# Input norm folded into the weights, x loaded early, query and key heads transposed in pairs, queries copied across partitions inside SBUF

## The chip, the cores and the metric

One NeuronCore of one Trainium2 chip. The metric is the device time of one launch in microseconds; a median over several runs is given where there are several.

## The reference

One layer of a hybrid decoder. The prompt has 2048 rows of 1024 (16 blocks of 128 rows); the sample batch adds 8 x 8 = 64 rows, treated as one more block (SB). All of it is float32.

```
h = rmsnorm(x, norm_in_g)             # per row, then times a gain per column
z = h @ w_in                          # 1024 x 3656, split into:
q, k, v, qi, ki, wi, ga, u, vm, gm
q, k = rope(rmsnorm(.)) per head      # 8 query heads, 4 key heads, 64 wide
qi, ki = rope(.)                      # indexer: 8 heads x 64, one key of 64
score = sum_h wi[h] * relu(qi[h] . ki)     # per query and key, causal
top 256 keys per query -> attention over them, times silu(ga)
gelu(u) * (spatial mix of layernorm(gelu(vm))) * silu(gm)
r = x + concat(.) @ w_out
y = r + sigmoid(rmsnorm(r) @ w_ple_gate) * (p @ w_ple_proj)
```

Returned are y for prompt and sample, and the new k, v, indexer keys and gated rows.

## The kernel before

Each float32 operand of a large product is split into a high half (float32r, rounded) and a low half (the rest), and a product is the sum of high x high, high x low and low x high.

**Phase A** makes the projections. `ROUNDS` groups the 17 blocks into three rounds of 6, 6 and 5; within a round the loop runs over the 14 column chunks of `CH` (x1, x2, vm0, vm1, k, v, ...), and within a chunk over the blocks. `load_w` (L264) brings a chunk's weights: in round 0 as eight raw pieces, each split into `whi` (GpSimd, for the first chunk every second one on ScalarE, L282 to L284) and `wlo` (L285: VectorE for the first six pieces, GpSimd for the last two), and both halves are then written to DRAM (L287); later rounds read the halves back (L273). `load_x` (L222) brings a block of x into one of two buffers; `norm_h` (L232) makes the sum of squares (ScalarE, L241), the inverse root (GpSimd, L242 and L243) and x times that times the gain (VectorE, L244); `split_h` (L246) transposes the normalised block in eight 128x128 tiles (L254) and splits it into `hhi` and `hlo` (`split`, L121: ScalarE copy, VectorE subtraction). `proj` (L301) runs 24 matmuls per prompt block and chunk, 16 for SB. `post` (L341) evacuates each chunk's result: indexer, query, key, value and gate parts, in part written to DRAM scratch (`s_qi`, `s_q`, `s_ga`). Between the blocks, `pump` (L446) feeds in the indexer: `idx` (L647) for a block of queries, with `load_qi` (L636), which loads each head's 64 columns twice side by side, so that a transpose puts the head on partitions 0 to 63 and again on 64 to 127. The key tile `ki_stack` holds the key's high half on partitions 0 to 63 and its low half on 64 to 127, so one matmul of 128 rows makes two of the three products. The scores are summed into a `big` tile that begins as a ramp made from `iota` (L663), and `topk` (L785) finds the threshold and writes a mask.

The end of phase A multiplies the gMLP part by half of w_out, and `prep_early` (L951) prepares attention beside it: keys are doubled on ScalarE (`twice`, L997), four transposes (L1005) and a split give `Kst`; `load_q` and `prep_q` do the same for queries (L1013), eight transposes (L1020).

**Phase B** is attention, block after block, four steps (pairs of heads) per block: scores (L1087, L1088), mask and minimum (L1089), exponential (L1096), transposes of the probabilities (L1122), their split, and the product with the values (L1139), with the sample block's attention woven in. `prep_q` of the next block follows a block's third step (L1212). **Phase C** is the output projection and the gate.

All loads and stores but the gathers go through one queue, SP's, in order. The order on each engine and queue is fixed before the run by the framework's planner (`schedule_with_timeline_sim=True`): it plays the program with estimated durations, and where an instruction isn't ready there, one that comes later in the program may go first. Each engine then runs its list in order. So the first ramp (`iota`, L491) stands in the trace ahead of the first norm, which the program has first.

## Time and profile before

| | |
|---|---|
| median of 3 runs | 1916.15 us (1910.57 to 1916.78) |
| profiled execution | 1912.54 us, span 1910.8 us |
| mean granted TensorE clock | 0.987 |
| TensorE busy | 1839.7 us, 96% |
| VectorE, ScalarE, GpSimd busy | 1254.9, 990.2, 632.3 us |
| moved by DMA | 262 MB, 137 GB/s in the mean |
| phase A, B, C end | about 1060, 1570, 1911 us |

The granted clock is 1.00 where TensorE has its upper level (2.4 GHz) and falls towards 0.5 (1.2 GHz) where it has the lower one. The busy time of TensorE holds the overlap of pipelined matmuls, so a mean of one matmul is longer than its share of the stream.

### The profile page before, as it was taken

What the parts mean: (1) busy time and instruction counts of PE and PEld (TensorE: products, weight loads), DVE (VectorE), ACT (ScalarE), POOL (GpSimd) and SP (SyncE); (2) the same over time, 40 slices, a digit from 0 to 9 for tenths busy, and PEclk for the clock granted to TensorE, in tenths of its full rate; (3) what the DMA queues carried; (4) which work ended last, traced back from release to release, by engine and by line L of the source; (5) the groups of instructions that cost most, each with busy time, mean ns of one, the idle gap of its engine ahead of it and who ended that gap; (6) DMA issues with size and microseconds to landing.
All of it is one profiled execution on the core that took longest, in us unless ns stands there. A gap on an engine that the chain in (4) does not pass through costs nothing. (4 is left out here: it accounts for less than half of the span.)

```text
span 1910.8 us, 34742 instructions
## 1 busy us (share of the span) xinstructions
PE 1839.7 (96%) x12374; PEld 1623.1 (85%) x12374; DVE 1254.9 (66%) x3612; ACT 990.2 (52%) x1909; POOL 632.3 (33%) x961
## 2 busy tenths in 40 slices
PE   5989998999999999999999899999999989999998
PEld 5989978999999999999998677778777777888887
DVE  5497745558779648788852689879888866233321
ACT  3234334345565625666764788868877653222221
POOL 4483563324003225005403443242222165222211
PEclk8999999999999999999999999999999999999999
DMA  8755666544444655445554433242322074222311
GB/s 256 226 155 179 197 197 219 182 128 144 130 145 157 222 159 163 149 147 163 168 191 150 133 105 89 65 119 65 82 61 65 20 267 133 85 95 94 103 36 45
DMA packets 242769, 262.10 MB, mean 137 GB/s; under 512 B 82136, under 2 KB 208672, under 8 KB 242208
## 3 DMA queue, kind: packets, MB, share of 16 engines
q1 hardware_dynamic: 236704, 240.97, 40.3%
q0 software_dynamic: 5888, 18.88, 3.3%
q8 instruction: 98, 1.61, 0.3%
q14 instruction: 79, 0.65, 0.1%
HBM read 172.42 MB, written 87.37 MB: 136 GB/s over the span
## 5 line engine op out<-in xcount | busy, mean ns | idle before, releaser
L314 PE MATMUL z<-whi,hhi 128*128 128x256 f32 (+1 forms) x1792 | 461.5, 291 | 11.6 <-ACT vt L408 3.6
L315 PE MATMUL z<-wlo,hhi 128*128 128x256 f32 (+1 forms) x1792 | 455.9, 288 | 1.9 <-POOL wlo L285 1.9
L314 PEld LDWEIGHTS z<-whi,hhi 128*128 128x128 f32 x1792 | 343.8, 192 | 19.9 <-issue 7.2
L315 PEld LDWEIGHTS z<-wlo,hhi 128*128 128x128 f32 x1792 | 344.2, 192 | 5.6 <-POOL wlo L285 2.4
L317 PE MATMUL z<-whi,hlo 128*128 128x256 f32 (+1 forms) x1792 | 270.3, 288 | 0.0
L317 PEld LDWEIGHTS z<-whi,hlo 128*128 128x128 f32 x1792 | 241.8, 191 | 4.2
L677 DVE SCALAR_TENSOR_TENSOR big<-dots,sgn,big 128x1024 f32<-128x1024 f32 (+7 forms) x176 | 179.3, 1019 | 58.0 <-ACT dots L675 56.9
L675 ACT ACTIVATE dots<-dots 128x1024 f32<-128x1024 f32 (+7 forms) x176 | 140.6, 802 | 109.1 <-PE dots L673 104.6
L124 DVE TENSOR_TENSOR b_pt<-b_tp,b_pt 128x512 fp32r<-128x512 f32 (+1 forms) x288 | 183.3, 656 | 11.8 <-ACT b_pt L123 10.2
L1139 PE MATMUL b_o<-b_pt,Vst 128*128 128x512 f32 x544 | 184.5, 424 | 0.9 <-DVE b_pt L124 0.7
L123 ACT ACTIVATE b_pt<-b_tp 128x512 fp32r<-128x512 f32 (+1 forms) x288 | 155.5, 579 | 47.6 <-PE b_tp L1122 41.6
L1122 PE MATMUL b_tp<-mats,b_sm 128*128 128x128 f32 x1088 | 170.6, 274 | 4.0 <-ACT b_sm L1096 2.7
L813 ACT ACTIVATE bfw<-big,tk 128x384 bf16<-128x384 f32 (+14 forms) x105 | 136.5, 1300 | 62.0 <-DVE tk L833 35.3
L1096 ACT ACTIVATE b_sm<-b_sm,b_st 128x128 f32<-128x128 f32 (+15 forms) x128 | 154.7, 1210 | 19.2 <-DVE b_st L1089 18.1
L1122 PEld LDWEIGHTS b_tp<-mats,b_sm 128*128 128x128 f32 x1088 | 132.4, 141 | 33.7 <-ACT b_sm L1096 6.9
L1087 PE MATMUL b_s<-Kst,b_qh 128*128 128x512 f32 (+3 forms) x320 | 140.2, 440 | 8.4 <-DVE b_st L1089 5.3
L1089 DVE CUSTOM_DVE_ANT_0 b_sm<-b_s,b_mask,b_st 128x512 f32<-128x512 f32 (+3 forms) x192 | 124.0, 646 | 25.9 <-PE b_s L1088 19.0
L1088 PE MATMUL b_s<-Kst,b_ql 128*128 128x512 f32 (+3 forms) x320 | 117.1, 369 | 0.0
L672 PE MATMUL dots<-ki_stack,qih 128*128 128x512 f32 (+3 forms) x304 | 111.6, 370 | 1.8 <-DVE big L677 1.8
L1139 PEld LDWEIGHTS b_o<-b_pt,Vst 128*128 128x128 f32 x544 | 90.1, 190 | 23.6 <-DVE b_pt L124 6.9
L673 PE MATMUL dots<-ki_stack,qil 128*128 128x512 f32 (+3 forms) x304 | 109.7, 371 | 0.0
L1449 PE MATMUL c_mm<-c_h_w_ple_gate,c_mh 128*128 128x512 f32 x272 | 109.0, 401 | 0.0
(347 smaller groups left out, 3847.1 us busy)
## 6 DMA issues: line engine op xcount, KB each, us to landing
whi<-s_wh SPq DMA_DIRECT2D x52, 512.0 KB
wlo<-s_wl SPq DMA_DIRECT2D x52, 512.0 KB
raw<-w_in SPq DMA_DIRECT2D x112, 128.0 KB
s_wh<-whi SPq DMA_DIRECT2D x13, 1024.0 KB
s_wl<-wlo SPq DMA_DIRECT2D x13, 1024.0 KB
x<-x_prompt SPq DMA_DIRECT2D x16, 512.0 KB
b_qr<-s_q SPq DMA_DIRECT2D x32, 256.0 KB
s_r<-hlo SPq DMA_DIRECT2D x32, 256.0 KB
```

The lines of the kernel that those rows point to most:

```text
L123: nc.scalar.activation(hi, src, AF.Copy)
L124: nc.vector.tensor_tensor(lo, src, hi.bitcast(F32), OP.subtract)
L314: nc.tensor.matmul(z, lhsT=hh[:, k], rhs=wh[:, k, :n], start=(k == 0), stop=False)
L315: nc.tensor.matmul(z, lhsT=hh[:, k], rhs=wl[:, k, :n], start=False, stop=False)
L317: nc.tensor.matmul(z, lhsT=hl[:, k], rhs=wh[:, k, :n], start=False, stop=(k == 7))
L675: nc.scalar.activation(r, r, AF.Relu)
L677: nc.vector.scalar_tensor_tensor(a, r, self.sgn[:, b, h:h + 1], a, op0=OP.mult, op1=OP.add)
L813: nc.scalar.activation(junk, acc[:P], AF.Sign, bias=cur[:, 0:1], accum_out=cur[:, 1:2])
L1087: nc.tensor.matmul(ps, lhsT=qh[:, h], rhs=rhs, start=True, stop=False)
L1096: nc.scalar.activation(part, part, AF.Exp, bias=stt[:, h, c:c + 1], scale=-1.0, accum_out=stt[:, h, 4 + e:5 + e])
L1122: nc.tensor.transpose(ps[:, k, r], sm2[r][:, (k0 + k) * 128:(k0 + k) * 128 + 128], ident)
L1139: nc.tensor.matmul(o.rearrange("p a b -> p (a b)"), lhsT=Vst[:, kb, g].rearrange("p a d -> p (a d)"), rhs=pt[:, k].rearrange("p a b -> p ( ...
```

## The change

- The gain of the input norm, `norm_in_g`, is loaded as `gk`, one column per 128 rows of w_in, and multiplied into the weights as they are split (GpSimd or ScalarE for the high half, VectorE for all low halves). x is transposed and split as it is. The sum of squares follows the split, and the inverse root `rs` per row is applied where results are evacuated (as the scale of the ScalarE operations in `post`). `norm_h` is gone.
- At the start, only the identity of the three constant matrices is loaded first. The six x blocks of round 0 are loaded early, two into the x buffers and four into `big` tiles; small constants and `page_rows` come later, gMLP's weights one chunk later; the write-back of weights waits until the third block of a chunk. There are six raw buffers in place of three. The weight tiles are packed to the chunk's width.
- In `idx`, `prep_q` and `prep_kv` two heads are transposed at once: one 128x128 tile gives an even head on partitions 0 to 63 and an odd one on 64 to 127. For queries, `heads` makes the high and low half on the head's own partitions and copies them to the other 64 by four SBUF-to-SBUF transfers on SP's queue. Keys are written to both places by ScalarE and VectorE. In `idx` transposes and copies stand before the first `yield`, so they are in the program one block ahead. `prep_q` moves from a block's third step to its first.
- The ramp of `idx` is made by GpSimd (`order`), as `iota` into the tile and a multiplication, and not from a kept 16-bit `iota`.

```diff
+        self.gk = const.tile([128, 8], F32, name="gk")
+        nc.sync.dma_start(self.gk, I["norm_in_g"][0].rearrange("(k p) -> p k", p=128))
...
-            rp = pool("a_raw", 3)
+            rp = pool("a_raw", 6)
...
-            def norm_h(b):
+            def split_h(b):
...
+                st = self.tiny.tile([128, 4], F32, name="hst")[:P]
+                rs = self.rs[:P, b:b + 1]
+                nc.scalar.activation(h, h, AF.Square, accum_out=st[:, 0:1])
+                nc.gpsimd.tensor_scalar(st[:, 1:2], st[:, 0:1], 1.0 / D, EPS, op0=OP.mult, op1=OP.add)
+                nc.gpsimd.tensor_tensor(rs, st[:, 1:2], self.mhalf[:P, 0:1], OP.pow)
+                nc.gpsimd.tensor_scalar(self.rs2[:P, b:b + 1], rs, rs, (8 * 64) ** -0.5, op0=OP.mult, op1=OP.mult)
...
+                    g = self.gk[:, k:k + 1]
+                    if ci == 0 and k % 2:
+                        nc.scalar.activation(wh[:, k], raw, AF.Copy, scale=g)
                     else:
-                        nc.gpsimd.tensor_scalar(wh[:, k, :n], raw[:, :n], 1.0, 1.0, op0=OP.mult, op1=OP.mult)
-                    (nc.vector if k < WLO_DVE[r] else nc.gpsimd).tensor_tensor(wl[:, k, :n], raw[:, :n], wh[:, k, :n].bitcast(F32), OP.subtract)
...
+                        nc.gpsimd.tensor_scalar(wh[:, k], raw, g, 1.0, op0=OP.mult, op1=OP.mult)
+                    nc.vector.scalar_tensor_tensor(wl[:, k], raw, g, wh[:, k].bitcast(F32), op0=OP.mult, op1=OP.subtract)
...
             W0 = load_w(0, 0)
-            norm_h(ROUNDS[0][0])
             split_h(ROUNDS[0][0])
+            load_x(ROUNDS[0][1])
...
+            for j in range(2, 6, 2):
+                t = big.tile([128, 2, D], F32, name="big")
+                for e in range(2):
+                    load_x(ROUNDS[0][j + e], t[:, e])
             for b in ROUNDS[0][1:]:
-                norm_h(b)
                 split_h(b)
...
+                    if r == 0 and j == 2:
+                        keep_w(c, cur)
...
+    def heads(self, pool, names, ps, bufs):
+        nc = self.nc
+        qh, ql = (pool.tile([128, 2, 4, 128], F32R, name=n, bufs=bufs) for n in names)
+        own = [slice(0, 64), slice(64, 128)]
+        for e in range(2):
+            nc.scalar.activation(qh[own[e], e], ps[own[e]], AF.Copy)
+            nc.vector.tensor_tensor(ql[own[e], e], ps[own[e]], qh[own[e], e].bitcast(F32), OP.subtract)
+        for t in (qh, ql):
+            for e in range(2):
+                nc.sync.dma_start(t[own[1 - e], e].bitcast(F32), t[own[e], e].bitcast(F32))
+        return qh, ql
...
-        qds = self.load_qi(b)
+        qd = wk2.tile([128, 4, 128], F32, name="qid", bufs=2)
+        nc.sync.dma_start(qd, self.s_qi[b].rearrange("p (h d) -> p h d", h=4))
+        ps = self.tp.tile([128, 4, 128], F32, name="tp")
+        for j in range(4):
+            nc.tensor.transpose(ps[:, j], qd[:, j], self.ident)
+        qh, ql = self.heads(wk2, ("qih", "qil"), ps, 2)
         yield None
...
-        nc.gpsimd.tensor_scalar(acc, self.iota[:, :W], -UNIT, 1.0, op0=OP.mult, op1=OP.mult)
+        self.order(acc, 128)
...
+            for j in range(2):
+                nc.tensor.transpose(ps[:, j], k[:, j * 128:j * 128 + 128], ident)
...
+                nc.scalar.activation(ks[own[e], :, e], ps[own[e], 0:2], AF.Copy)
+                V.tensor_tensor(ks[own[1 - e], :, e], ps[own[e], 0:2], ks[own[e], :, e].bitcast(F32), OP.subtract)
...
-                if si < len(steps) and g == 2 and at + 1 < NB:
+                if si < len(steps) and g == 0 and at + 1 < NB:
                     self.prep_q(ORDER[at + 1], psum)
```

## Rows read from the trace of the kernel before

**Rows 1.** The page's first part: busy time, share of the span and instructions of the engines.

```profile
PE 1839.7 (96%) x12374; PEld 1623.1 (85%) x12374; DVE 1254.9 (66%) x3612; ACT 990.2 (52%) x1909; POOL 632.3 (33%) x961
```

**Rows 2.** Stretches of the span: from and to (us), length, busy time and instructions of TensorE, its weight loads, VectorE, ScalarE and GpSimd, then the granted clock, the share of the DMA engines and GB/s.

```profile
0.00:20.00 20.00, 8.10 (x33) 7.24 (x34) 9.16 (x23) 8.43 (x14) 6.58 (x17) 0.91 0.75 227
20.00:40.00 20.00, 14.88 (x82) 14.22 (x81) 11.71 (x32) 5.83 (x17) 12.53 (x23) 0.74 0.86 291
40.00:60.00 20.00, 15.62 (x95) 14.48 (x94) 11.60 (x31) 5.66 (x20) 8.26 (x23) 0.83 0.75 232
60.00:80.00 20.00, 20.00 (x168) 19.16 (x167) 9.14 (x27) 2.51 (x8) 13.31 (x37) 1.00 0.71 214
...
120.00:160.00 40.00, 34.91 (x230) 30.35 (x229) 35.59 (x144) 16.44 (x46) 30.53 (x44) 0.91 0.54 165
...
300.00:400.00 100.00, 94.39 (x706) 92.38 (x706) 46.34 (x161) 36.61 (x86) 28.09 (x72) 0.95 0.63 202
...
600.00:700.00 100.00, 95.07 (x743) 93.84 (x742) 65.50 (x246) 47.76 (x101) 29.06 (x64) 0.98 0.56 181
...
1300.00:1400.00 100.00, 99.48 (x637) 79.15 (x636) 89.91 (x242) 80.57 (x153) 26.05 (x44) 1.00 0.26 73
```

**Rows 3.** Groups of instructions, the transposes of query and key heads: line, engine, operation, out<-in, shapes, count; busy us, mean ns of one; idle time before them and what ended it.

```profile
L1020 PE MATMUL b_tp<-mats,b_qr 128*128 128x128 f32 x120 | 17.7, 273 | 0.7 <-DVE b_pt L124 0.7
L657 PE MATMUL tp<-mats,qid 128*128 128x128 f32 x112 | 17.2, 273 | 0.0
...
L1005 PE MATMUL tp<-mats,b_kd 128*128 128x128 f32 x64 | 9.8, 273 | 1.1 <-DVE Kst L1008 1.1
```

**Rows 4.** The order of time in phase B, TensorE: start (us), length from first start to last end, engine, line, operation, count. Eight transposes of one block's queries and what follows them.

```profile
1075.82 1.04 PE L1020 MATMUL b_tp<-mats,b_qr 128*128 128x128 f32 x8
1076.62 0.49 PE L1139 MATMUL b_o<-b_pt,Vst 128*128 128x512 f32 x1
```

**Rows 5.** Groups of instructions, two subtractions of VectorE on 128 and on 64 partitions, as in rows 3.

```profile
L124 DVE TENSOR_TENSOR b_ql<-b_tp,b_qh 128x512 fp32r<-128x512 f32 x30 | 20.2, 685 | 1.0 <-ACT b_qh L123 0.8
...
L1008 DVE TENSOR_TENSOR Kst<-tp,Kst 64x512 fp32r<-64x512 f32 x16 | 11.0, 695 | 32.6 <-ACT Kst L1007 32.5
```

**Rows 6.** The order of time in the first 60 us, as in rows 4; in brackets the idle time before and what ended it.

```profile
0.85 1.84 POOL L491 IOTA iota<- 128x2048 int16 x1 [0.40 <-POOLq L1557]
...
1.20 0.42 SPq L226 DMA_DIRECT2D x<-x_prompt  x1
...
2.13 2.81 SPq L279 DMA_DIRECT2D raw<-w_in  x6
...
4.86 1.06 ACT L241 ACTIVATE hhi<-x 128x1024 fp32r<-128x1024 f32 x1 [2.85 <-DMA x<-x_prompt]
...
8.13 1.28 DVE L244 SCALAR_TENSOR_TENSOR x<-x,hst,gb 128x1024 f32<-128x1024 f32 x1 [4.89 <-DMA gb<-norm_in_g]
...
8.59 1.58 POOL L284 TENSOR_SCALAR whi<-raw 128x328 fp32r<-128x328 f32 x2 [1.65 <-DMA raw<-w_in]
...
9.47 1.97 PE L254 MATMUL tp<-mats,x 128*128 128x128 f32 x8 [9.47 <-DMA raw<-w_in]
...
26.15 1.02 POOL L686 DMA_INDIRECT sraw<-cache_idx_k,prow  x1 [0.18 <-issue]
...
27.20 1.71 POOL L285 TENSOR_TENSOR wlo<-raw,whi 128x328 fp32r<-128x328 f32 x2
...
28.97 0.64 PE L315 MATMUL z<-wlo,hhi 128*128 128x328 f32 x1 [1.95 <-POOL wlo L285]
...
37.70 1.36 PE L317 MATMUL z<-whi,hlo 128*128 128x328 f32 x8
38.90 0.31 PE L314 MATMUL z<-whi,hhi 128*128 128x328 f32 x1
...
58.07 0.28 PE L314 MATMUL z<-whi,hhi 128*128 128x256 f32 x1
```

**Rows 7.** What TensorE waited for in the first 60 us: who waited for whom, us in total, times, longest.

```profile
PE tp L254 <- DVE x L244: 6.1, 2, 3.2
...
PE z L315 <- POOL wlo L285: 1.9, 1, 1.9
```

**Rows 8.** Groups of instructions, the low halves of the weights on VectorE and on GpSimd, as in rows 3.

```profile
L285 DVE TENSOR_TENSOR wlo<-raw,whi 128x256 fp32r<-128x256 f32 (+1 forms) x84 | 41.7, 510 | 26.1 <-POOL whi L284 25.3 <-issue 0.7
...
L285 POOL TENSOR_TENSOR wlo<-raw,whi 128x256 fp32r<-128x256 f32 (+1 forms) x28 | 21.3, 768 | 1.4
```

**Rows 9.** The page's third part: the DMA queue of SP, with its packets, MB, and the time of its packets as a share of 16 engines' span.

```profile
q1 hardware_dynamic: 236704, 240.97, 40.3%
```

**Rows 10.** The instructions on the tile of the indexer's queries: the loads on SP's queue, with the shortest, median and longest time of an issue (ns).

```profile
L643 SPq DMA_DIRECT2D qid<-s_qi x60: 359/498/1904, 55.7 to 801.0; - x60
```

**Rows 11.** What SP's queue waited for, over the span, as in rows 7: the store of one attention block's result.

```profile
SPq L1174 <- POOL b_ga L1172: 224.6, 15, 56.4
```

**Rows 12.** The order of time at the start of phase B, as in rows 6: the first scores of block 1 and of block 2, and SP's loads of the sample block's mask.

```profile
1068.96 0.55 PE L1087 MATMUL b_s<-Kst,b_qh 128*128 128x256 f32 x1 [0.95 <-ACT b_qh L123]
...
1069.21 5.72 SPq L1275 DMA_DIRECT2D s_m<-s_mask  x11
...
1078.21 0.62 PE L1087 MATMUL b_s<-Kst,b_qh 128*128 128x384 f32 x2
```

**Rows 13.** Groups of instructions, the projections' first matmuls, as in rows 3.

```profile
L314 PE MATMUL z<-whi,hhi 128*128 128x256 f32 (+1 forms) x1792 | 461.5, 291 | 11.6 <-ACT vt L408 3.6 <-DVE kin L134 2.7 <-ACT whi L282 2.3
```

More of the change, by code (lines that the diff above doesn't have):

```diff
@@ L649, in idx @@
         W = 128 * (b + 1)
-        qds = self.load_qi(b)
-        yield None
-        qh, ql = [], []
-        for j in range(2):
-            qd = qds[j].rearrange("p h a d -> p h (a d)")
-            ps = self.tp.tile([128, 4, 128], F32, name="tp")
-            for h in range(4):
-                nc.tensor.transpose(ps[:, h], qd[:, h], self.ident)
-            qh.append(wk2.tile([128, 4, 128], F32R, name="qih", bufs=3))
-            ql.append(wk2.tile([128, 4, 128], F32R, name="qil", bufs=3))
-            self.split(qh[j], ql[j], ps)
-            yield 2
+        qd = wk2.tile([128, 4, 128], F32, name="qid", bufs=2)
[4 more added lines that the diff above has]
+        qh, ql = self.heads(wk2, ("qih", "qil"), ps, 2)
+        yield None
         acc = self.big.tile([128, SEQ], F32, name="big")[:, :W]
-        nc.gpsimd.tensor_scalar(acc, self.iota[:, :W], -UNIT, 1.0, op0=OP.mult, op1=OP.mult)
+        self.order(acc, 128)
         kf = self.ki.rearrange("p a b -> p (a b)")
@@ L691, in sample_idx @@
         V = nc.vector
-        qi = wk2.tile([128, 4, 128], F32R, name="qih", bufs=3).bitcast(F32)
+        both = wk2.tile([128, 2, 4, 128], F32R, name="qih", bufs=2).bitcast(F32)
+        qi = both[:, 0]
         nc.gpsimd.memset(qi, 0.0)
@@ L708, in sample_idx @@
         gt = wk2.tile([128, 4, 2, 64], F32, name="qid", bufs=2).rearrange("p h a d -> p (h a d)")[:64]
-        pick = wk2.tile([128, 4, 128], F32R, name="qih", bufs=3)
-        pick = pick.bitcast(F32).rearrange("p a b -> p (a b)")[:64, 0:64].rearrange("p (a b) -> p a b", a=8)
+        pick = both[:64, 1, 0, 0:64].rearrange("p (a b) -> p a b", a=8)
         nc.sync.dma_start(pick, I["c_pick"])
@@ L729, in sample_idx @@
         acc = self.big.tile([128, SEQ], F32, name="big")
+        self.order(acc[:, :WS], 64)
         pgs = {}
@@ L764, in sample_idx @@
                     f()
+                t = wk2.tile([128, 2, 4, 128], F32R, name="qil", bufs=2).bitcast(F32)
+                kT, rr = t[:, 0].rearrange("p a b -> p (a b)"), t[:, 1].rearrange("p a b -> p (a b)")[:, :n]
                 if c < 2:
@@ L979, in load_q @@
         def load_q(i):
-            q = io.tile([128, 8, 2, 64], F32, name="b_qr", bufs=1)
+            q = io.tile([128, 4, 128], F32, name="b_qr", bufs=1)
             ga = io.tile([128, 512], F32, name="b_ga")
-            for a in range(2):
-                nc.sync.dma_start(q[:, :, a], self.s_q[i].rearrange("t (h d) -> t h d", h=8))
+            nc.sync.dma_start(q, self.s_q[i].rearrange("t (h d) -> t h d", h=4))
             nc.sync.dma_start(ga, self.s_ga[i])
@@ L1014, in prep_q @@
             q, ga = qs.pop(i)
-            qh = qp.tile([128, 8, 128], F32R, name="b_qh")
-            ql = qp.tile([128, 8, 128], F32R, name="b_ql")
-            for j in range(2):
-                ps = psum()
-                for h in range(4):
-                    nc.tensor.transpose(ps[:, h], q[:, j * 4 + h].rearrange("p a d -> p (a d)"), ident)
-                self.split(qh[:, j * 4:j * 4 + 4], ql[:, j * 4:j * 4 + 4], ps)
+            ps = psum()
+            for j in range(4):
+                nc.tensor.transpose(ps[:, j], q[:, j], ident)
+            qh, ql = self.heads(qp, ("b_qh", "b_ql"), ps, 2)
             stt = tiny.tile([128, 8, 6], F32, name="b_st")
@@ L1081, in scores, with chunk @@
                     out.append(sm)
-                    def chunk(c, h=h, sm=sm):
+                    def chunk(c, h=h, sm=sm, r=r):
                         c0, cn = c * 512, min(512, W - c * 512)
```

171 lines of the change are left out of this document (78 added, 93 removed).

## The prediction

> **What bounds the kernel now.** I read the page's busy times first, then stretches of the span, then what TensorE waits for, and last the places that the change touches. TensorE is busy 96% of the span and no other compute engine is over 66% [rows 1], so time comes off in two ways only: less work on TensorE, or less of the stretches where it stands still or runs at a low clock. The worst stretch is the start: in the first 60 us TensorE is busy 8.1, 14.9 and 15.6 of 20 us, 38.6 in all, at granted clocks of 0.91, 0.74 and 0.83, so it moves between its two levels [rows 2]. Two smaller gaps lie at the round boundaries, and in phase B VectorE is also close to full: 89.9 us of 100 beside TensorE's 99.5 [rows 2].
>
> The profiled execution took 1912.54 us around a span of 1910.8; the median of the runs shown is 1916.15 (1910.57 to 1916.78). My sum is made against 1912.5 and the forecast is set a little above it.
>
> **Transposes.** idx() transposes 4 tiles for a block in place of 8, over 14 blocks (2 to 15): 56 gone. prep_q the same over 16 blocks: 64 gone. prep_kv 2 in place of 4 over 16: 32 gone. With the sample block's ki_t: 153. A transpose shows as 273 ns [rows 3], but these overlap: eight take 1.04 us from first start to last end, and the next matmul starts 0.80 us after the first of them [rows 4]. So one costs the stream 0.10 us, 0.13 at most. 153 x 0.10 = 15.3 us, upper end 153 x 0.13 = 19.9. 93 of them lie in phase A, where TensorE has little slack: 93 x 0.10 = 9.3 us, counted whole. 60 lie in phase B (6.0 us), where VectorE keeps the same work: halving the partitions of an operation doesn't shorten it, as a 64x512 subtraction takes 695 ns and a 128x512 one 685 [rows 5], so the new 64-partition copies and subtractions of heads() cost what the old ones did. I count half, 3 us, and the low end is nothing. Together 12.3 us, between 9.3 and 19.9.
>
> **Start.** The pass over x1 holds 48 transposes and 5 x 24 + 16 = 136 matmuls of 328 columns. At full clock eight of the latter take 1.20 us (37.70 to 38.90) [rows 6], 0.15 each, so the pass is 48 x 0.13 + 136 x 0.15 = 26.6 us of work, but it ends where x2 begins, at 58.07 [rows 6]: 31 us are lost. The rows say to what. The first transpose waits to 9.47 for x to be normalised, although x was there at 4.86, because the gain landed late (L244 began at 8.13 after VectorE had waited for it) [rows 6]. Later blocks wait 6.1 us on L244 again [rows 7]. And a last low half of the first chunk comes from GpSimd at 27.20, behind an indirect load, which lets TensorE on at 28.97 only [rows 6].
>
> After the change no transpose waits for a norm, only for x and the identity: start at about 5.7 (4.86 and two more issues of some 0.4). SP's issues are the next limit: 16 pieces of the first chunk at 0.47 (six took 2.81) [rows 6], from 2.6 to 10.1; the last lands 3.7 us later (x: issued 1.20, used 4.86 [rows 6]), 13.8, and is split by 15.1 (0.79 for a high half on GpSimd [rows 6], some 0.5 for a low half on VectorE [rows 8]). All low halves are on VectorE now, and six raw buffers in place of three keep the queue moving. Block 0's last ten matmuls, at half clock and so 0.3 each, end at 18.1. Then five blocks are left: 40 x 0.13 + 112 x 0.15 = 22.0 us, so the pass ends at 40.1, 18 us before 58.07. Their x tiles have no buffer to wait for: 2.4 MB behind the weights at 227 to 291 GB/s [rows 2] are there by about 24, and block 5 is wanted at 36. Moving the weights' write-back to the third block of a pass takes 2.7 MB out of this stretch. I take 15 us, as the order is the planner's and the next chunk's pieces queue behind five x loads. Ends: 6.1 (only the waits on L244 go [rows 7]) and 58.07 - 5.7 - 26.6 = 25.8.
>
> One part of the start could turn it over: gk, 1024 single elements gathered from norm_in_g, which now gates every split of the first round. In this profile a packet costs 0.403 x 16 x 1910.8 us / 236704 = 52 ns of an engine [rows 9]. Over 16 engines 1024 of them take 3.3 us, and gk is there before 8.59, when the first raw piece was [rows 6]: no loss. The Trainium skill speaks against such a load (DMA: Bandwidth & Descriptors, "Rules for kernel authors"): a strided last dimension is lowered to one descriptor per element, and one should rearrange so that it is contiguous. No row of this profile shows such a load; the rule weighs for the rival on gk below, whose time is worked out there from rows.
>
> **Round boundaries.** In the 100 us around each of the two, TensorE stands 5.6 and 4.9 us, at clocks of 0.95 and 0.98 [rows 2]. The change takes 1.28 us of VectorE per block (L244 [rows 6]) from before the transposes; the Square on ScalarE stays, behind them, and gates only the evacuation. I take 3 us for both, between 0 and 10.5.
>
> **What it adds.** (a) Copies between partition halves: 4 transfers per block, 30 blocks. Price of one set: four issues of 0.50 (median [rows 10]) and 3.7 us to land, 5.7. In idx they are issued a whole block ahead; in prep_q, from the third block on, three of a block's four steps ahead, so other work hides them. Not so in blocks 1 and 2: block 1's scores wait already for b_qh at 1068.96, while SP issues 11 mask loads from 1069.21 in 5.7 us, and block 2's begin at 1078.21, nine us later [rows 12]. I take 3 us for both; ends 0 and 11.4. (b) SP's queue: behind a copy that waits for VectorE stand the loads and stores after it. SP already stands 56.4 us behind one store of s_o [rows 11], and TensorE is busy throughout, since the rest is loaded a block ahead: nothing. (c) idx's transposes now stand right behind their load in program order. TensorE's order is fixed beforehand by the planner, which fills with projections: nothing, at worst 14 x 3.7 = 52 us. (d) GpSimd makes the ramp by an iota too (1.84 us for 2048 columns [rows 6]) per block; it is at 33% [rows 1]. Only at 120 to 160, where VectorE is busy 35.6 of 40 us and GpSimd 30.5 [rows 2], could it matter: there GpSimd loses two low halves per chunk (0.77 each) and VectorE gains them (0.51 each [rows 8]). Even: nothing, between 4 lost and 3 gained. (e) Larger packets for stored weights: nothing, as the projections wait on weights for 2.3 us only, all in the first chunk's splits [rows 13]. (f) The ScalarE copies of twice() go: nothing, they lie beside TensorE.
>
> **Sum.** 12.3 + 15 + 3 - 3 = 27.3: 1912.5 - 27.3 = 1885.2. Against the shown median I say 1886.
>
> **Rivals.** *The start's gain is partly eaten*, because the first passes run on VectorE, GpSimd and DMA rather than on TensorE: for it, VectorE's 35.6 of 40 us at 120 to 160 and a DMA share of 0.75 to 0.86 in the first 60; against, TensorE's 20.0 of 20 at 60 to 80 [rows 2]. Then 12.3 + 6.1 + 0 - 3 = 15.4 gained: 1897. *Everything comes in*: 19.9 + 20 + 6 = 46 gained, 1866; for it, the 31 us lost at the start [rows 6]. *Slower, by late queries*: the planner's estimate of the load in idx or of the copies is shorter than what the chip takes, and TensorE, in order, stands at a transpose or a score. There are 44 places (14 loads, 30 copies); it cancels the 30 us gained elsewhere at 0.7 us each, and at 1.4 us each gives 1912.5 - 30 + 62 = 1944. For it: the wait at 1068.96 [rows 12]; against: no transpose of queries waits for its load in this profile [rows 3]. *gk on one engine*: 1024 x 52 ns = 53 us before the first split [rows 9], 44 us after the 8.59 of now, and 15 us are saved elsewhere: 1912.5 + 44 - 15 = 1941. *It doesn't do what it says*: the planner puts the x loads behind the weights and the start stays, phase B absorbs its share, and the waits of blocks 1 and 2 take the rest: 9.3 - 9, 1912.
>
> **Chances.** Forecast 0.55; partly eaten 0.17; everything 0.13; late queries 0.08; gk 0.02; no effect 0.05. A difference of 0.3% (5.7 us) is about what a measurement of this kernel can tell from no change. Faster 0.86, same 0.05, slower 0.09. The range reaches from the case where everything comes in to the one where the start is partly eaten and the copies show at 7 us more: 1866 to 1904.
>
> **What would show it.** Right: x2's first matmul at about 40 us; 56 transposes of qid, 64 of b_qr and 32 of keys gone from the counts; the waits on L244 gone; TensorE's busy share still 96% or more. Wrong: TensorE waiting for qih, qil, b_qh or b_ql by more than 10 us in all; the first weight split later than 10 us with gk as its releaser; VectorE as releaser for more than 15 us between 60 and 200.

## The result, and the profile after

The changed kernel takes 1927.53 us (median of 4 runs, 1926.77 to 1930.3) beside 1914.41 us of the kernel before on the same chip: a ratio of 1.0077, with an interval of 1.0063 to 1.009. It is slower by 0.8%; the prediction was 1886 and faster. Its profiled execution has a span of 1925.2 us, 14.4 more than before. The page's first part, which answers to [rows 1]:

```profile
PE 1836.9 (95%) x12221; PEld 1612.7 (84%) x12221; DVE 1250.1 (65%) x3638; ACT 1015.9 (53%) x1908; POOL 641.4 (33%) x965
```

Stretches of the span, with the columns of [rows 2], and two more at the end of phase A:

```profile
0.00:20.00 20.00, 13.53 (x59) 11.01 (x60) 8.23 (x27) 8.00 (x16) 6.32 (x20) 1.00 0.85 234
20.00:40.00 20.00, 14.51 (x93) 12.58 (x92) 12.98 (x39) 9.89 (x26) 12.92 (x30) 0.89 0.88 285
40.00:60.00 20.00, 14.79 (x88) 14.06 (x88) 8.27 (x28) 2.43 (x9) 10.10 (x27) 0.85 0.78 258
...
300.00:400.00 100.00, 97.92 (x773) 96.76 (x772) 42.83 (x164) 42.31 (x92) 30.05 (x80) 1.00 0.66 216
600.00:700.00 100.00, 98.88 (x777) 97.50 (x776) 56.90 (x229) 49.77 (x100) 29.35 (x65) 1.00 0.61 197
950.00:1000.00 50.00, 41.85 (x343) 41.21 (x341) 27.77 (x97) 31.59 (x41) 0.55 (x1) 0.95 0.65 210
1000.00:1050.00 50.00, 39.38 (x306) 38.09 (x307) 19.22 (x54) 17.31 (x40) 17.79 (x32) 0.88 0.40 129
```

The last two stretches in the kernel before:

```profile
950.00:1000.00 50.00, 49.69 (x419) 49.48 (x420) 29.18 (x105) 31.19 (x43) 2.61 (x5) 1.00 0.54 181
1000.00:1050.00 50.00, 45.56 (x384) 44.44 (x383) 15.10 (x34) 23.90 (x45) 18.07 (x32) 1.00 0.51 161
```

153 matmuls are gone, as counted. TensorE stands less at the start and at both round boundaries, but at the end of phase A it stands 18.8 us of 100 where it stood 4.8. So work was saved, and came out as waiting. To see where, three times are read from the order of time on TensorE: the first score of attention (phase A ends), the last one (phase B), and the end. This table has them for all runs below, with two numbers that the argument needs: when SyncE stored block 15's indexer scores, and how long scores waited for copied query halves (the releasers "DMA b_qh" and "DMA b_ql").

| kernel | block 15 stored | phase A | phase B | rest | waits for copies in B | span |
|---|---|---|---|---|---|---|
| before | 959.2 | 1060.4 | 478.0 | 372.4 | - | 1910.8 |
| changed | 961.8 | 1061.7 | 489.5 | 374.0 | 10.3 | 1925.2 |
| e1 queries as before | 965.1 | 1062.3 | 477.5 | 383.6 | - | 1923.4 |
| e2 keys as before | 964.4 | 1063.9 | 478.8 | 372.2 | 0.9 | 1914.8 |
| e3 one-step ramp | 950.3 | 1054.7 | 484.1 | 379.1 | 7.7 | 1917.9 |
| e4 four index keys | 953.9 | 1053.4 | 480.8 | 375.1 | 1.4 | 1909.3 |
| e5 copies by ScalarE | 963.6 | 1064.1 | 485.0 | 378.5 | 4.3 | 1927.6 |
| e6 = e3 + e4 | 946.3 | 1049.4 | 490.4 | 379.2 | 11.3 | 1919.0 |
| e7 = e2 + e3 + e4 | 945.4 | 1048.9 | 475.9 | 379.1 | 2.2 | 1903.8 |
| e8 start alone | 949.9 | 1053.6 | 476.7 | 374.2 | - | 1904.5 |
| e9 start with room | 936.3 | 1043.6 | 475.8 | 372.5 | - | 1891.9 |
| e10 keys later | 941.7 | 1037.3 | 476.7 | 375.5 | - | 1889.5 |
| e11 indexer pairs with room | 947.0 | 1050.2 | 478.0 | 372.5 | - | 1900.7 |
| e12 ramp in two | 959.8 | 1063.4 | 477.8 | 384.0 | - | 1925.2 |
| e13 query pairs on e10 | 941.4 | 1037.6 | 483.3 | 373.4 | 5.0 | 1894.3 |

Each row is one profiled execution. Runs of one kernel lie 2.5 us (e5) to 17.5 us (before) apart, so a difference of a few us between two rows can be chance; e9's profile is the fastest of its six runs, 5.8 us under their median.

The 14.4 us of the change are 1.2 in phase A, where 27.3 were to be gained, 11.6 in phase B and 1.6 in the rest.

**The start.** The second chunk begins at 50.25, where 40.1 was forecast and 58.07 was before [rows 6]. The longest wait of all engines between 30 and 60 us, then SyncE in order of time, the shortest, median and longest issue of `w_s` (ns) with SyncE's longest wait there, and TensorE in order of time:

```profile
ACT kin L358 <- DMA idx_k_prompt<-kin: 11.8, 2, 6.3
```

```profile
39.05 0.36 SPq L361 DMA_DIRECT2D idx_k_prompt<-kin  x1
...
42.49 7.51 SPq L628 DMA_DIRECT2D big<-w_s  x8
50.11 0.28 SPq L636 DMA_DIRECT2D big<-b_s  x1
50.44 0.36 SPq L231 DMA_DIRECT2D x<-x_prompt  x1
50.91 0.37 SPq L361 DMA_DIRECT2D idx_k_prompt<-kin  x1
```

```profile
L628 SPq DMA_DIRECT2D big<-w_s x8: 273/336/845, 42.5 to 49.7; - x8
SPq L628 <- DMA s_wl<-wlo: 2.1, 1, 2.1
```

```profile
50.25 0.36 PE L319 MATMUL z<-whi,hhi 128*128 128x256 f32 x1 [1.72 <-DVE vt L316]
55.59 0.36 PE L319 MATMUL z<-whi,hhi 128*128 128x256 f32 x1 [2.23 <-ACT kin L358]
```

The index key `kin` has two buffers. ScalarE fills a third one only after a store has freed the first. The first of its two waits, 6.3 us, ends when the store of 39.05 has landed, 5.7 us after its issue. The second, 5.5 us, ends with the store of 50.91, which stands behind eight issues of `w_s` that hold SyncE 7.51 us. The issues themselves take 0.27 to 0.85 us; about half of the 7.51 us SyncE waits for earlier transfers to land, longest for a low half of weights on its way to DRAM. While ScalarE waits, `z` is not evacuated, and TensorE stands.

**The end of phase A.** TensorE's longest wait from 940 to 1060, and its place:

```profile
PE tp L1020 <- DVE Kst L1025: 14.4, 1, 14.4
```

```profile
1006.20 0.69 PE L1020 MATMUL tp<-mats,b_kr 128*128 128x128 f32 x2 [14.35 <-DVE Kst L1025]
```

A key transpose needs one of two PSUM buffers; VectorE frees them by the subtraction L1025, and VectorE is at block 15's top-k and the flag until 1004.86. The products of the gMLP part stand behind the transpose on TensorE. In every kernel of the table phase B begins 96 to 107 us after block 15's scores are stored.

Where the gain of the start went is read from the stores of block 12's and of block 15's scores, before and then changed:

```profile
798.75 0.45 SPq L798 DMA_DIRECT2D s_score<-big  x1
959.21 0.90 SPq L798 DMA_DIRECT2D s_score<-big  x1
```

```profile
791.73 0.34 SPq L820 DMA_DIRECT2D s_score<-big  x1
961.79 0.34 SPq L820 DMA_DIRECT2D s_score<-big  x1
```

Block 12 is still 7.0 us early. From there to block 15 it takes 160.5 us before and 170.1 changed. In the nine kernels with the indexer's heads in pairs these three blocks take 170.1 to 171.4 us with the ramp in two operations and 162.8 to 164.5 with one (e3, e6, e7, e11); with eight transposes it is 159.9 to 164.6, and 165.8 in e12, the only one of these six with two operations.

**Block 4 in phase B.** All engines in order of time, from block 3's last score and the transposes of block 4's queries to block 4's first score:

```profile
1104.38 0.39 PE L1098 MATMUL b_s<-Kst,b_qh 128*128 128x512 f32 x1
...
1104.85 0.60 PE L1034 MATMUL b_tp<-mats,b_qr 128*128 128x128 f32 x4
...
1106.65 0.61 ACT L666 ACTIVATE b_qh<-b_tp 64x512 fp32r<-64x512 f32 x1
...
1107.79 0.32 SPq L1005 DMA_DIRECT2D b_ga<-s_ga  x1
1107.85 0.98 POOL L707 DMA_INDIRECT s_pg<-cache_k,prow  x1 [2.39 <-DMA s_o<-b_ga]
...
1108.20 0.47 SPq L670 DMA_DIRECT2D b_qh<-b_qh  x1
...
1113.76 0.77 PE L1098 MATMUL b_s<-Kst,b_qh 128*128 128x512 f32 x1 [6.19 <-DMA b_qh<-b_qh]
```

The transposes stand behind block 3's last score and not three steps ahead of block 4. The copy of `b_qh` is ready for its issue at 1107.26, waits on SyncE behind the load of the gate, and then lands late.

### The profile page after: what moved, and what is told of

The parts are those of the page before. It is cut to its first block, busy times and chain, and to the rows that moved or that the text cites. A ratio compares the mean times of both kernels' runs of the same rounds, so it can differ in the third digit from the quotient of the medians.

```text
span 1925.2 us, 34688 instructions
## 1 busy us (share of the span) xinstructions
PE 1836.9 (95%) x12221; PEld 1612.7 (84%) x12221; DVE 1250.1 (65%) x3638; ACT 1015.9 (53%) x1908; POOL 641.4 (33%) x965
```

## The experiments

Runs e1 to e7 edit the changed kernel, e8, e9 and e12 the kernel before, and e10, e11 and e13 what their texts say. Each ratio is to the kernel before on the same chip, with its 95% interval; that of the changed kernel is 1.0077.

**e1: queries as before.** `load_q`, `prep_q` and the place of `prep_q` (third step) are those before.

```diff
-            for j in range(4):
-                nc.tensor.transpose(ps[:, j], q[:, j], ident)
-            qh, ql = self.heads(qp, ("b_qh", "b_ql"), ps, 2)
+            for j in range(2):
+                ps = psum()
+                for h in range(4):
+                    nc.tensor.transpose(ps[:, h], q[:, j * 4 + h].rearrange("p a d -> p (a d)"), ident)
+                self.split(qh[:, j * 4:j * 4 + 4], ql[:, j * 4:j * 4 + 4], ps)
```

> The changed kernel, with the attention queries alone prepared as in the kernel before (each head loaded twice, eight transposes, one split over 128 partitions, no transfers inside SBUF, prepared in a block's third step). Theory 1 (the changed kernel's phase B loses its time at scores that wait for the copied halves in blocks 2 to 4): the time from the first score to the last, 489 us in the changed kernel and 478 before, comes back to 478 to 481, no score waits for b_qh by a DMA, and the median falls by 8 to 12 us from 1927.5, to about 1917. Rival (phase B is longer because it begins at a lower clock with VectorE behind, whatever prepares the queries): the stretch stays at 486 us or more and the median within 3 us of 1927.5.

Measured: 1926.03 us, 1.0057 (1.0044 to 1.0071). Phase B took 477.5, as theory 1 says, but the time after it grew by 9.6 us, although the edit is not there. The total alone would have told against a theory that the stage bears out; e12 takes this up.

**e2: keys as before.** `twice` and four transposes.

```diff
-            for j in range(2):
-                nc.tensor.transpose(ps[:, j], k[:, j * 128:j * 128 + 128], ident)
+            for g in range(4):
+                nc.tensor.transpose(ps[:, g], k[:, g].rearrange("p a d -> p (a d)"), ident)
```

> The changed kernel, with the attention keys alone prepared as before (a doubled copy on ScalarE, four transposes, one copy and one subtraction). Theory 1 (TensorE's 14.4 us at a key transpose around 1000 us come from where the planner puts the transposes ahead of the last products while VectorE is still at the last block's top-k; the end of phase A is set by that top-k and the sixteen key blocks behind it, not by how a key block is made): a wait of 8 us or more stays there, the first score of phase B stays within 3 us of 1061.7, the median within 4 us of 1927.5. Rival (the two copies and two subtractions of 64 partitions in place of one each are the cost): the first score comes 5 us earlier or more, and the median falls by as much.

Measured: 1918.76 us, 1.0027 (1.0016 to 1.0037). Phase B began at 1063.9, so the key blocks' form isn't what sets the end of phase A. The median fell by 9 us all the same, which neither theory had: phase B took 478.8, with the query copies still there and only 0.9 us of waits for them. Block 4 here:

```profile
1101.56 0.33 SPq L1005 DMA_DIRECT2D b_ga<-s_ga  x1
...
1102.64 0.60 PE L1038 MATMUL b_tp<-mats,b_qr 128*128 128x128 f32 x4
...
1105.97 0.47 SPq L670 DMA_DIRECT2D b_qh<-b_qh  x1
...
1108.21 0.50 PE L1105 MATMUL b_s<-Kst,b_qh 128*128 128x512 f32 x1 [0.35 <-DMA b_qh<-b_qh]
```

The load of the gate went out 4.4 us ahead of the copy, not 0.4, and the copy was usable 2.24 us after its issue, not 5.56. A gather of GpSimd, issued 0.35 us ahead of the copy in the changed kernel, went out 0.83 us behind it here. The planner had put the same instructions in another order; which of the transfers ahead of the copy makes it late was not tried.

**e3: ramp in one operation.** The ramp is written as integers whose bits read as tiny falling floats.

```diff
-        nc.gpsimd.iota(acc[:P], pattern=[[1, acc.shape[1]]], base=0, channel_multiplier=0,
-                       allow_small_or_imprecise_dtypes=True)
-        nc.gpsimd.tensor_scalar(acc[:P], acc[:P], -UNIT, 1.0, op0=OP.mult, op1=OP.mult)
+        nc.gpsimd.iota(acc[:P].bitcast(I32), pattern=[[1, acc.shape[1]]], base=(17 << 23) - (1 << 31), channel_multiplier=0)
```

> The changed kernel, with the ramp in the score tile written by GpSimd in one operation (an integer ramp in the tile's bits, which read as floats is again tiny, negative and falling) in place of two. Theory 1 (block 15's indexer slipped because its ramp's second operation ran 6.2 us after the first, behind weight splits on GpSimd): block 15's scores are stored at about 954 in place of 961.8, phase B begins 5 to 8 us earlier than 1061.7, the median falls to 1920 to 1923. Rival (block 15 is held by something else, or the end of phase A does not follow it): the store stays at 960 or later, or it comes earlier and phase B still begins within 2 us of 1061.7; the median stays within 3 us of 1927.5.

Measured: 1919.92 us, 1.0025 (1.001 to 1.004). Block 15 was stored at 950.3, phase B began 6.9 us earlier: theory 1. That the median fell as forecast is in part chance: phase B was 5.5 us shorter too, and the rest 5.2 longer. GpSimd at block 15's hand-over, changed kernel first, then e3:

```profile
897.84 1.85 POOL L657 IOTA big<- 128x2048 f32 x1 [12.53 <-DVE v L871]
...
901.77 2.25 POOL L302 TENSOR_SCALAR whi<-raw 128x256 fp32r<-128x256 f32 x6 [0.94 <-PE z L322]
904.10 1.92 POOL L659 TENSOR_SCALAR big<-big 128x2048 f32<-128x2048 f32 x1
```

```profile
890.01 1.84 POOL L657 IOTA big<- 128x2048 int32 x1 [6.56 <-DVE v L869]
```

Weight splits of w_out stood between the two halves of the ramp. From block 14's store to block 15's it is 62.4 us in the changed kernel (899.4 to 961.8), 58.0 in e3, 53.6 before.

**e4: four buffers of the index key.**

```diff
-                    kin = wk.tile([128, 64], F32, name="kin")[:P]
+                    kin = wk.tile([128, 64], F32, name="kin", bufs=4)[:P]
```

> The changed kernel, with four buffers in place of two for the index key (kin), which ScalarE fills for each block of the first chunk and SyncE stores. Theory 1 (the start's gain is lost because ScalarE waits 11.8 us for the stores of earlier index keys, which stand on SyncE behind eight 0.94 us issues of w_s, and TensorE then waits for the buffers of z): the wait goes, the second chunk's first matmul moves from 50.25 to 44 us or less, and 8 us or more of matmuls are ahead of the changed kernel by 60 us. If the end of phase A follows TensorE's work, the median falls by 5 to 8 us; if it follows the last block's indexer and top-k whose place the planner sets, the median moves by less than 3 us. Rival for the start (the buffers of z are held by the vector work of the post step, not by the stores): the second chunk still starts at 48 us or later.

Measured: 1914.44 us, 0.9994 (0.9982 to 1.0006). The wait for the store is gone, the second chunk begins at 43.00, and the gain is kept to block 15's store (7.9 us earlier) and to the end of phase A (8.2), although the stand of 14.4 us at a key transpose is still there. So time gained early does reach the end, and the branch in which the last block's top-k eats it falls. Of the 15.9 us of the profiled span 8.2 are phase A and 8.8 phase B, where again the waits for copies fell (1.4), by another order; the rest gave 1.1 back. The 0.94 us an issue in the text above is 7.51 divided by eight, SyncE's waits included.

**e5: copies issued by ScalarE.**

```diff
-                nc.sync.dma_start(t[own[1 - e], e].bitcast(F32), t[own[e], e].bitcast(F32))
+                (q or nc.sync).dma_start(t[own[1 - e], e].bitcast(F32), t[own[e], e].bitcast(F32))
```

> The changed kernel, with the transfers of the attention queries between the partition halves issued by ScalarE in place of SyncE; the indexer's stay on SyncE. The runs so far have given stage lengths: phase B, from its first score to its last, takes 478.0 us before, 489.5 changed, and less the time that scores wait there for copied halves it is 476 to 479 in every run. Theory 1 (the copies are late because on SyncE they stand behind a load of the gate that waits for the store of an earlier block, and then land behind those loads): waits for b_qh and b_ql by a DMA fall from 10.3 us to 4 or less, phase B takes 478 to 483, the median falls by 6 to 11 us from 1927.5. Rival (landing is what is slow, whoever issues, or the copies take ScalarE's time instead): phase B stays at 486 us or more, or grows by ScalarE's issues.

Measured: 1929.89 us, 1.0096 (1.0081 to 1.0111). Waits fell to 4.3 and phase B by 4.5, half of what theory 1 says; the other stages took it back. At block 2 the copies were issued at 1077.67 and 1079.35 with nothing ahead of them on that queue, beside GpSimd's gathers and SyncE's loads, and the score began at 1083.00. So SyncE's order is a part, landing another. The Trainium skill (DMA: Bandwidth & Descriptors, "Issuing engines are not separate DMA queues") says that transfers of all issuing engines share the same 16 DMA engines and interleave, so that another issuer saves the issuing alone; the copy of 1077.67, usable only 5.3 us after its issue, agrees.

**e6: e3 and e4 together.** Both diffs above.

> The changed kernel with both earlier edits of phase A: the ramp in one operation, and four buffers for the index key. Theory 1 (phase A ends some 100 us after block 15's scores are stored, and each of the two brings that store forward by a cause of its own, 11.5 us for the ramp and 8 for the buffers): block 15's scores are stored at 942 to 946 in place of 961.8, phase B begins at 1042 to 1049, and the median is 1908 to 1914. Rival (both took the same slack away, or a bound of TensorE's work stands in the way): the store comes no earlier than 950 and phase B begins at 1053 or later. In phase B the order of SyncE's transfers is that of the changed kernel, so waits for copied halves of 5 us or more are expected by theory 1 to return there.

Measured: 1923.38 us, 1.006 (1.0044 to 1.0075). Phase B began at 1049.4, 12.3 us earlier and 0.4 past the forecast; the two alone gave 6.9 and 8.2, so they don't add up fully. Phase B returned to 490.4 with 11.3 us of waits, as said from SyncE's order. The rest grew by 5.3. Of the 12.3 us 6.2 are left in the profiled span, and the median misses its window by 9 us.

**e7: e6 with the keys as before.** The diffs of e2, e3 and e4.

> The changed kernel with the ramp in one operation, four buffers for the index key, and the attention keys prepared as before. Theory 1: phase A ends as in the run with the first two edits (phase B begins at 1042 to 1049); in phase B the gate's loads stand less often between the copies in SyncE's order than in the changed kernel, so the waits for copied halves are under 4 us and phase B takes 478 to 482. Median 1900 to 1906, which is faster than before by 0.4% to 0.7%. Rival (the end of phase A is set by the key blocks' own chain, which undoing their pairing makes longer): phase B begins at 1052 or later, the median at 1912 or more.

Measured: 1910.26 us, 0.9997 (0.9985 to 1.0009). Phase A as in e6, phase B 475.9 with 2.2 us of waits: theory 1 for both stages, phase B 2 us under its window. The total misses its window by 4 us or more, because the rest took 379.1.

**e8: the start alone, on the kernel before.** The change's hunks up to the order of the first round; `kin` stays doubled, heads, keys, queries and ramp as before. Of its diff against the kernel before:

```diff
-            norm_h(ROUNDS[0][0])
             split_h(ROUNDS[0][0])
+            load_x(ROUNDS[0][1])
...
-                    nc.scalar.activation(kin2, z[:, None, 0:64].to_broadcast([P, 2, 64]), AF.Copy)
+                    nc.scalar.activation(kin2, z[:, None, 0:64].to_broadcast([P, 2, 64]), AF.Copy, scale=rs)
```

> The kernel before with only the change's first part: the norm folded behind the transposes, early loads of x, all low halves of the first round on VectorE, six raw buffers, larger packets for kept weights; heads, keys and ramp stay as before. Theory 1 (the start itself gains, but little, because ScalarE stands at stores of index keys behind the w_s issues): the second chunk starts between 48 and 53 us in place of 58.1, block 15's scores are stored 3 to 8 us before 959.2, phase B takes 477 to 480, and the median is 3 to 8 us under the kernel before. Rival (the first part alone is what slows block 15's indexer, the ramp being innocent): the store of block 15's scores comes at 960 or later and the median is not under that of before.

Measured: 1904.86 us, 0.9962 (0.9948 to 0.9977): faster. Phase A gains 6.8 us, and ScalarE waits 11.8 us for stores of `kin` here too. So of the changed kernel's parts this one gains, and everything else together costs some 20 us.

**e9: e8 with the ramp of e3 and six buffers of the index key.**

```diff
-        nc.gpsimd.tensor_scalar(acc, self.iota[:, :W], -UNIT, 1.0, op0=OP.mult, op1=OP.mult)
+        self.order(acc, 128)
...
-                    kin2 = wk.tile([128, 2, 64], F32, name="kin")[:P]
+                    kin2 = wk.tile([128, 2, 64], F32, name="kin", bufs=6)[:P]
```

> The kernel before with the change's start alone (as in the run of the start alone), plus the one-operation ramp in the tile's bits, which needs no table of indices, and the room of that table given to six buffers of the index key. Heads, keys and queries as before. Theory 1 (the start was held by stores of index keys that stand on SyncE, and a gain there reaches block 15's scores and so the end of phase A): the second chunk starts at 43 to 46 us in place of 51.4, block 15's scores are stored at 941 to 945 (949.9 with the start alone), phase B begins at 1045 to 1049 and takes 476 to 479, the median is 1896 to 1901. Rival (what the start gains beyond the start alone is lost before block 15): the store stays at 948 or later and the median at 1903 to 1907.

Measured: 1899.44 us, 0.9934 (0.9919 to 0.9949). The second chunk begins at 44.72, block 15 is stored at 936.3 and phase B begins at 1043.6: more than theory 1 asked. With its stores out of the way and the ramp of e3 the start is worth 16.8 us of phase A; the share of the ramp is not separated.

**e10: key blocks four products later, on e9.**

```diff
-EARLY = 15
+EARLY = 19
```

> The kernel of the run before this one, with the key blocks of phase B offered to the planner four products later (EARLY 19 in place of 15). Theory 1 (TensorE, in order, stands at key transposes because VectorE, still at the last block's top-k, holds their buffers; with the products put ahead of them it works through that time): the wait at the key transposes goes, TensorE's idle time between 950 and 1050 falls by 5 us or more, phase B begins 3 to 8 us earlier than in that run. Rival (the end is set by the sixteen key blocks' own chain of loads, splits and the flag behind the top-k, so that offering them later only delays it): phase B begins as late or later, by up to 10 us, and the median is not lower.

Measured: 1891.92 us, 0.9891 (0.9875 to 0.9907), the fastest kernel here, 1.1% under before and, by the two ratios, 1.8% under the changed one. It is 7.5 us under e9 by the medians, 2.4 by the profiled spans. Phase B begins 6.3 us earlier than in e9, although block 15 is stored 5.4 us later. TensorE from 950 to near the end of phase A, e9 and then e10:

```profile
950.00:1000.00 50.00, 47.50 (x386) 46.47 (x385) 22.84 (x79) 27.92 (x42) 9.36 (x18) 0.97 0.47 151
1000.00:1040.00 40.00, 34.18 (x261) 33.20 (x262) 10.18 (x16) 16.08 (x31) 8.60 (x15) 0.91 0.36 119
```

```profile
950.00:1000.00 50.00, 49.27 (x415) 49.03 (x414) 22.38 (x85) 27.66 (x41) 4.83 (x10) 1.00 0.50 161
1000.00:1037.00 37.00, 34.38 (x286) 33.33 (x286) 10.95 (x18) 18.12 (x36) 13.01 (x23) 1.00 0.44 142
```

It stands 3.4 us in place of 8.3 and its clock no longer falls: products now fill the time of the last top-k.

**e11: the indexer's pairs, with the start and its room.** The changed kernel with the diffs of e1 to e4: keys and queries as before, ramp in one operation, four index keys.

> The changed kernel with the one-operation ramp, four buffers of the index key, and attention keys and queries both as before: against the kernel with the start and the same ramp it differs by the indexer's paired heads alone (four transposes and four transfers a block in place of eight transposes). Theory 1 (the 56 transposes saved, 5.6 us of TensorE, do not bring block 15's scores forward, and its hand-over from block 14 is longer with pairs, 58 to 59 us from store to store in place of 53 to 54): block 15's scores are stored at 942 to 947, no earlier than in that kernel, phase B takes 476 to 479 with no wait for copies, and the median is within 5 us of that kernel's. Rival (the transposes saved count in full): the store comes 5 us or more ahead of that kernel's, and the median is lower by as much.

Measured: 1903.62 us, 0.9953 (0.9937 to 0.997). Against e9, which has the eight transposes, phase A is 6.6 us longer. The hand-over from block 14 to 15 takes 59.7 us in place of 55.0, but that isn't the reason: from block 12 to block 15 both take 164 us, and block 12's scores are stored 10.6 us later here (782.54 beside 771.99). The pairs in the indexer gain nothing here. That they cost is not shown: the medians differ by 0.2% and their intervals overlap, another order alone moved these stores by 5 us (e9 to e10), and the two kernels also make the index key differently (four buffers of 64 columns, six of 128). Why the transposes saved don't show stays open.

**e12: the kernel before with the ramp in two operations.**

```diff
-        nc.gpsimd.tensor_scalar(acc, self.iota[:, :W], -UNIT, 1.0, op0=OP.mult, op1=OP.mult)
+        nc.gpsimd.iota(acc, pattern=[[1, W]], base=0, channel_multiplier=0, allow_small_or_imprecise_dtypes=True)
+        nc.gpsimd.tensor_scalar(acc, acc, -UNIT, 1.0, op0=OP.mult, op1=OP.mult)
```

> The kernel before, with the ramp alone written in two operations, as in the changed kernel. Theory 1 (the second operation, which the planner lets stand behind other GpSimd work, delays each block's scores, block 15's by 5 to 8 us): block 15's scores are stored at 963 to 968 in place of 959.2, phase B begins 4 to 8 us later than 1060.4 and takes 477 to 479, and the median is 4 to 8 us over that of before. Rival (GpSimd, busy for a third of the span, has room for it, and the delay in the changed kernel came with the paired heads): the store is within 2 us of 959.2 and the median within 2 us of before.

Measured: 1928.86 us, 1.0081 (1.0055 to 1.0107). The sum looks like theory 1 and more, but the stages deny it: block 15's store is 0.6 us later and phase A 3.0 longer; the hand-over did grow, from 53.6 to 57.8, after an earlier block 14. The other 11.6 us lie behind phase B, where there is no ramp. The stretch 1550 to 1600, before and e12:

```profile
1550.00:1600.00 50.00, 45.67 (x214) 36.64 (x215) 35.15 (x29) 20.28 (x30) 32.67 (x23) 1.00 0.74 260
```

```profile
1550.00:1600.00 50.00, 39.87 (x171) 30.34 (x170) 33.76 (x28) 18.61 (x29) 33.30 (x23) 0.89 0.74 260
```

SyncE at this place, before and then e12:

```profile
1543.26 2.67 SPq L1394 DMA_DIRECT2D c_raw<-w_ple_gate  x2
1545.98 1.36 SPq L1413 DMA_DIRECT2D c_mix<-s_o  x1
```

```profile
1545.88 6.41 SPq L1395 DMA_DIRECT2D c_raw<-w_ple_gate  x3
1552.34 0.42 SPq L1414 DMA_DIRECT2D c_mix<-s_o  x1
```

In six kernels (e1, e3, e5, e6, e7, e12) three pieces of w_ple_gate stand ahead of the first load of `c_mix`, and the rest takes 378.5 to 384.0 us; in the other nine it is two pieces, and 372.2 to 375.5. That the third piece is the cause is read from this split and was not tried by itself.

**e13: the queries in pairs alone, on e10.** The reverse of e1's diff, with `heads`:

```diff
-                if si < len(steps) and g == 2 and at + 1 < NB:
+                if si < len(steps) and g == 0 and at + 1 < NB:
```

> The kernel of the run with the key blocks four products later, with the attention queries in pairs as in the changed kernel (four transposes, four transfers on SyncE, in a block's first step) and nothing else of the pairing. Theory 1 (a set of transposes and transfers takes 5.6 us or more from the first transpose to a score that can use it, TensorE has 3 to 5 us of other work there in blocks 2 to 4, so the pairs lose by themselves): phase A and C stay within 2 us of that run's 1037.3 and 375.5, phase B takes 479 to 490 in place of 476.7, by as much as scores wait for copies, and the median is 2 to 12 us over 1891.9. Rival (pairs lose only by the order around them in the changed kernel, and 64 transposes saved are worth 3 to 6 us): phase B takes 471 to 475 and the median is 1886 to 1890.

Measured: 1896.71 us, 0.9916 (0.9899 to 0.9934). Phases A and rest as in e10 within 2.1 us, phase B 483.3 in place of 476.7, with these waits for copies over phase B:

```profile
PE b_s L1108 <- DMA b_ql<-b_ql: 2.7, 3, 2.0
PE b_s L1107 <- DMA b_qh<-b_qh: 2.3, 3, 1.9
```

Theory 1: the pairs of queries lose by themselves, 4.8 us by the medians (on two chips, with intervals that overlap) and 6.6 in phase B. Without its 5.0 us of waits phase B would be 478.3, so the 64 transposes saved don't show.

## Why the prediction was wrong

**Transposes, -12.3.** The count was right; the groups that answer to [rows 3]:

```profile
L1034 PE MATMUL b_tp<-mats,b_qr 128*128 128x128 f32 x60 | 9.5, 283 | 0.0
L680 PE MATMUL tp<-mats,qid 128*128 128x128 f32 x56 | 8.6, 272 | 0.0
L1020 PE MATMUL tp<-mats,b_kr 128*128 128x128 f32 x32 | 6.4, 283 | 16.5 <-DVE Kst L1025 14.4 <-DMA b_kr<-k_prompt 2.2
```

The step that failed is "93 of them lie in phase A, where TensorE has little slack ... counted whole". Phase A ends some 100 us behind block 15's scores, and these came 2.6 us later, not 9 earlier. A busy share of 96% was read as no slack, without asking which chain ends the stage: the last block's indexer, its top-k, then key blocks in an order that lets TensorE stand (14.4 us at one transpose). Phase A is not slack throughout, as e4's 8.2 us reach its end. But in the changed kernel block 12 was 7.0 us early, no more than the start alone explains, and 9.6 us were lost from there to block 15, of which e3 gives back 7.3. e11 shows no gain from the 56 of the indexer, and why is open. In phase B the seven kernels with old queries take 477.2 us in the mean, and the eight with pairs, their waits taken off, 478.1: there too nothing.

**Start, -15.** The mechanism was right: the first transpose ran at 5.96 (forecast 5.7), no transpose waited for a norm, and e9, with six buffers of the index key, gains 16.8 us. In the changed kernel the term was about twice what came: the second chunk began at 50.25 and not at 40.1, 7.8 us earlier than before. The failed step is "Then five blocks are left: ... 22.0 us", which counts TensorE's work alone and has no term for the evacuation of `z`; (b), which weighs what stands behind copies on SP's queue, says "nothing". ScalarE waited 11.8 us for two stores, and e4, with four buffers, begins the second chunk at 43.00. The prediction looked for loads that come late, and not for stores that free a buffer. e8's 6.8 us lie at its lower end, 6.1.

**gk.** The first high half on GpSimd, at 8.59 before [rows 6], began at 6.52, released by a raw piece and not by gk; that rival is out, and the rule of the Trainium skill that the prediction weighs for it (DMA: Bandwidth & Descriptors, "Rules for kernel authors") has no visible price here:

```profile
6.52 0.54 POOL L288 TENSOR_SCALAR whi<-raw,gk 128x328 fp32r<-128x328 f32 x1 [5.45 <-DMA raw<-w_in]
```

**Round boundaries, -3.** TensorE stands 2.1 and 1.1 us there where it stood 5.6 and 4.9: 7.3 us, inside the stated 0 to 10.5. It didn't reach the end either.

**Copies, +3.** The price of a set, forecast at 5.7 us, is 5.6 us from the first transpose to block 4's first score in e2 and in e4, but 8.9 in the changed kernel, where the copy lands later. The failed step is "three of a block's four steps ahead, so other work hides them": a step of an early block is short, the planner lets the transposes stand behind the last score of the block before, and at block 4 the planner's order leaves TensorE only 2.7 us (changed kernel) to 5.2 (e2) of work between the transposes and the score. 10.3 us of waits answer to the 11.4 of the upper end, which reckoned with blocks 1 and 2; they fell on blocks 2, 3 and 4, so the agreement is chance. Phase B follows, and with the queries as before (e1) the 11.6 us are gone: in all fifteen kernels it takes 473.7 to 480.7 us plus these waits.

**(d) the ramp, "Even: nothing".** It was weighed at 120 to 160, by busy shares. It mattered at a hand-over, where a second operation stands behind other work on an engine that is busy a third of the span: 6.9 us of phase A (e3). On the kernel before (e12) phase A grew by 3.0, but block 15's store by 0.6 only, so there it is not shown.

**The rivals.** "Slower, by late queries" named the right kind of place and the right sign, at 0.08. It had 44 places and 30 us gained elsewhere to cancel; there were four waits of 10.3 us in all, none of them for the indexer's copies or loads, and the gains elsewhere had not reached the end of phase A. Of the prediction's own signs of being wrong one came, by a hair: waits for copies of "more than 10 us in all".

## What to carry to other kernels

A saving on the busiest engine counts only if the chain that ends the stage gets shorter: find that chain (here the last block's indexer and top-k) before multiplying instructions by their price, and let the saved time have work to do there, as e10 does. When transfers are added or moved, ask which buffers the stores behind them free, and take the lead of a copy in microseconds at the smallest block. Where a planner orders the program, compare stage by stage: an edit changes the order at places it doesn't touch, by up to 12 us here, and a total then confirms or denies a theory by chance (e1, e12).

## What the runs showed of the hardware

A copy of 128 KB between partition halves of SBUF was usable 2.24 us after its issue where two loads of 192 and 256 KB had been issued 2.3 and 2.7 us before (e2, block 4). It was usable only 5.56 us after its issue where a third load of 256 KB went out 0.41 us and a gather 0.35 us before it (changed kernel, block 4). At the eight issues of `w_s` in the changed kernel SyncE was held 7.51 us, of which the issues took 3.5. Its longest waits there were for transfers issued eight places earlier on its queue: the issue of 47.30 for that of 40.33, the issue of 49.73 for that of 40.80. And a stand of TensorE costs more than its length: in the changed kernel's 18.8 us between 950 and 1050 the granted clock fell to 0.95 and 0.88, towards its level of 1.2 GHz, where e10, standing 3.4 us up to 1037, kept 1.00.
